# An encoder trunk on one core: bias reads moved in a queue, factors in two parts, wider products in two places

## The chip, the core and the metric

The kernel runs on one core of a Trainium2 chip. The core's engines work side by side, each through its own queue of instructions in a fixed order: TensorE (PE, products; its weight loads are listed as PEld), VectorE (DVE), ScalarE (ACT), GpSimd (POOL) and SyncE (SP), which issues nearly all transfers. Engines wait for each other by semaphores. Products write to eight banks of 128×512 fp32; everything else works in an on-chip memory of 128 partitions. The metric is the device time of one execution in microseconds, the median over runs.

## The reference

512 tokens of 1024 channels pass through two layers, each a mixer and an MLP, each with a norm ahead and a residual behind it, all in fp32, and then a last RMSNorm.

```python
for i in range(DEPTH):                      # two layers
    h = h + mixer_i(rms_norm(h, g_mix[i]))
    h = h + (relu(rms_norm(h, g_mlp[i]) @ w_in[i]) ** 2) @ w_out[i]     # 1024 -> 4096 -> 1024
out = rms_norm(h, norm_final_g)
```

Mixer 0 is attention in dilated windows: 16 heads of 64 channels in three groups (6 heads with dilation 1, 5 with 4, 5 with 16), with a bias by relative position. Each head's output is multiplied, token by token, by a factor that depends on the log-sums of all three groups, and then by w_o. Mixer 1 is differential attention: 8 heads with two softmaxes over all 512 keys, whose difference weights v; then a norm per head and w_o.

## The kernel before

**Products.** Every large product is made of three in a reduced fp32 form: both operands are split into a high and a low part, and `mm3` (L167 to L169) adds hi·hi, hi·lo and lo·hi. The activations lie with channels on the partitions, the 512 tokens along the columns. In `linear_steps` a 128×128 block of weights is held and 512 tokens stream past it. Where the tokens are to end up on the partitions (layer 1's v in `values1`, and `m_end`, the last chunk of the last MLP) it is the other way round: 128 tokens are held and 256 columns of weights stream.

**Weights** come in units of 1 MB, 128 × 8 × 256 or 128 × 4 × 512. `fetch` issues one transfer on SP (L153), casts it in two halves to the high part on ACT (L156, `whi`), and subtracts for the low part on DVE (L157, `wlo`). The raw, high and low tiles have two buffers each; `next_w` hands out one unit and fetches the next. The units' order is one list for the whole program. The first two units come in sixteen small loads (L316, L321), one per 128 channels as x arrives. While these are on their way PE computes idle products of an identity (L130, `WARM` of them).

**Order.** Each engine's order is set when the program is built, by a scheduler that follows the program and its dependences; `tc.high_priority()` moves work ahead and `tc.issue_after(x)` keeps an instruction behind another.

**Layer 0.** The bias lies as one row per head in a table `fd` in DRAM, and `hankel` (L425) reads it with overlapping rows: B0 for the 6 heads of the first group (128×6×256), B1 for the 10 others. `softmax_block` (L475 on DVE adds the bias and finds the minimum, L477 on ACT the exponential) follows the logits. Heads go in pairs, p = 0 to 7; pairs 0 to 2 make logits in split form (L349, L350), pairs 3 to 7 ("class logits", L493) from the 64 rows of one head each, `lo64` and `hi64`, four blocks to a head. `values0` makes v and the weighted sums (L541 to L555, O). The sums of the groups go through DRAM and back (L617, L618, `exS`, `allN`), `head_factors` makes a factor per head and token, one transposition brings them to 64 rows (L624, L626), they are written to DRAM (L627, `fac`) and read back spread over 64 partitions per head (L633, `fB`). L641 multiplies O by them, L649 and L650 split the result (`oh`, `ol`), and w_o follows.

**Layer 1.** `qk1` and `values1` make q, k and v, two heads at a time (j = 0 to 3). `woven` steps through the attention of the heads (`attend1`) and takes 1.5 steps of `fill`, the q, k and v of later heads, per step. An attention block of 128 queries: logits, L816 (DVE) and L819 (ACT) softmax, the difference, transpositions (L835), a copy to `aT` (L837, ACT), and the product with v (L844); there are 8 × 4 blocks. `wo1_first` and `wo1_last` apply w_o (b_w_o) in two parts of heads.

**The last stage.** `m_end` turns h to tokens on partitions (L716), adds the products per 256 columns and 128 tokens (L724), squares and sums (L726), multiplies by the norm's gains (L728; on POOL for the first three quarters, `gB`), and in the last quarter adds the four sums (L731, L732), takes the power −1/2 on POOL (L734), scales (L736 on ACT, L738 on DVE) and writes out (L737, L739).

Of the kernel before, what the change touches and what calls it, by code (L numbers as in the profile page):

```python
# [14 lines left out]
ALU = mybir.AluOpType  # L15
# [13 lines left out]
WARM = 14  # L29
# [53 lines left out]
def tile_encoder(ctx: ExitStack, tc: tile.TileContext, x, rel_bias, gains, norm_final_g,  # L83
# [57 lines left out]
    units, ready = [], []  # L141
# [4 lines left out]
    def fetch():  # L146
# [6 lines left out]
        nc.sync.dma_start(raw, w[r0:r0 + kt * P, c0:c0 + ncol].rearrange("(k p) c -> p k c", p=P))  # L153
        for i in range(2):
            c = slice(i * ncol // 2, (i + 1) * ncol // 2)
            nc.scalar.copy(hi[:, :, c], raw[:, :, c])  # L156
            nc.vector.tensor_sub(lo[:, :, c], raw[:, :, c], f32(hi[:, :, c]))  # L157
# [13 lines left out]
    def linear_steps(ct0, kt, ncol, xs, on_out, bank=None, hooks=(), hold=None):  # L171
# [8 lines left out]
        for c in range(ncol // P):  # L180
            s = slice(c * P, (c + 1) * P)
            ps = (bank or acc_tile)()
            for k in range(kt):
                mm3(ps, hi[:, k, s], lo[:, k, s], xh[k], xl[k], k == 0, k == kt - 1)
                n += 1
                if n in hooks:
                    hooks.pop(n)()
                yield
# [99 lines left out]
    for j in range(4):  # L288
        for part in range(3):
            qkv_unit(b_w_qkv, part, j)  # L290
# [157 lines left out]
    hankel(B0, 0, 6, E_G0 + 64, 256)  # L448
# [150 lines left out]
    hankel(B1[:, 0:5, :], 6, 5, E_G1, P)  # L599
    hankel(B1[:, 5:10, :], 11, 5, E_G2, P)  # L600
# [18 lines left out]
    head_factors(allS, [(sS, 0, 5, 1), (sS, 5, 10, 2)])  # L619
    head_factors(allN, [(sN, 0, 6, 0)])  # L620

    fac = dram.tile([64, P], F32, name="fac")
    T = t_tile()
    nc.tensor.transpose(T[0:64, 0:P], sA.rearrange("p h b -> p (h b)"), ident)  # L624
    fT = l0p.tile([64, P], F32, name="fT", bufs=1)
    nc.scalar.copy(fT, T[0:64, 0:P])  # L626
    nc.sync.dma_start(fac, fT)  # L627
    F = []
    for pp in range(4):
        f = l0p.tile([P, 2, SEQ], F32, tag="ptn", name="fB", bufs=4)  # L630
        for hh, rows in enumerate((lo64, hi64)):
            a = fac[0:1, 0:1]
            nc.sync.dma_start(f[rows], bass.AP(tensor=a.tensor, offset=a.offset + (4 * pp + hh) * SEQ,  # L633
                                               ap=[[0, 64], [2 * SEQ, 2], [1, SEQ]]))
        F += [f[:, 0, :], f[:, 1, :]]
# [3 lines left out]
    oh_, ol_ = [], []  # L639
    for p in range(8):  # L640
# [10 lines left out]
        oh_.append(hi)  # L651
        ol_.append(lo)
# [9 lines left out]
    for c in range(4):  # L662
        run(linear_steps(2 * c, KT, 256, (oh_, ol_), on, bank=wide))
# [4 lines left out]
    def mlp(i, nm, nxt, last=False):  # L668
# [32 lines left out]
        def m_end(c):  # L701
# [6 lines left out]
            for q in range(4):  # L708
                cs = slice(q * 256, (q + 1) * 256)
                hi, lo = next_w()  # L710
                for half in range(2):
                    T = t_tile().rearrange("p (u c) -> p u c", u=2)
                    for u in range(2):
                        for e in range(2):
                            b = 2 * half + u
                            nc.tensor.transpose(T[:, u, e * P:(e + 1) * P], hT[2 * q + e][:, b * P:(b + 1) * P], ident)  # L716
                    nc.scalar.copy(hN[:, 2 * half:2 * half + 2, cs], T)
                for b in range(NB):
# [4 lines left out]
                    h = hN[:, b, cs]  # L723
                    nc.vector.tensor_add(h, h, ps)  # L724
                    sq = mp.tile([P, 256], F32, tag="sqN", name="sqN")
# [271 lines left out]
```

## Time and profile before

| | |
|---|---|
| runs | 1213.69 us median of 3 (1213.35 to 1214.45) |
| profiled execution | 1211.44 us, span 1209.7 us |
| mean granted clock of TensorE | 0.997 |
| busy | PE 1191.5, PEld 1005.9, DVE 629.3, ACT 500.8, POOL 87.4 us |
| transfers | 117.85 MB, 97 GB/s over the span |

A row of a group or of the timeline has the start (or none), the time, the engine, the line, the operation, and its output and inputs by name; in square brackets stands how long the engine had been idle before it and what it waited for. Products overlap, so the start of one to the start of the next tells what one costs, not its own duration. "Granted clock" is the share of full speed that TensorE was given.

### The profile page before, as it was taken

To read this page: it belongs to the slowest core of one execution; us is meant where nothing else is said; L and a number is where in the kernel's file an instruction comes from. 1 tells how busy PE (TensorE), PEld (TensorE's weight loads), DVE (VectorE), ACT (ScalarE), POOL (GpSimd) and SP (SyncE) were. 2 spreads that over 40 slices of the span, in tenths; PEclk is the share of its full clock that TensorE was granted. 3 is DMA by queue.
4 is the path that set the end of the run, shared out by engine and by line. 5 is a ranking of instruction groups with operands and counts; after the bars stand their busy time and mean duration, and the time that the engine had idled before them with its cause. 6 is when DMAs were issued, how large, how long until landed. Compare 5 with 4: busy or idle time off the path is not lost.

```text
span 1209.7 us, 15193 instructions
## 1 busy us (share of the span) xinstructions
PE 1191.5 (99%) x6093; PEld 1005.9 (83%) x6093; DVE 629.3 (52%) x1052; ACT 500.8 (41%) x923; POOL 87.4 (7%) x145
## 2 busy tenths in 40 slices
PE   9999999999999999999999999999999999999997
PEld 7788877888888888888888898987888888888897
DVE  5684465744433434335478668675644344334333
ACT  5462434534412313313367667655444133123133
POOL 0000000300000000001101121213200000000012
PEclk9999999999999999999999999999999999999999
DMA  7632124333233322333432233222323332233311
GB/s 227 118 105 58 57 72 131 105 105 97 79 103 105 105 80 94 105 105 99 121 105 89 86 123 101 72 80 85 96 82 104 105 105 83 91 105 105 100 41 70
DMA packets 108710, 117.85 MB, mean 97 GB/s; under 512 B 4847, under 2 KB 101295, under 8 KB 108591
## 3 DMA queue, kind: packets, MB, share of 16 engines
q1 hardware_dynamic: 108576, 116.61, 30.9%
q8 instruction: 48, 0.79, 0.3%
q0 software_dynamic: 64, 0.27, 0.1%
q14 instruction: 22, 0.18, 0.1%
HBM read 114.60 MB, written 2.27 MB: 97 GB/s over the span
## 4 chain that ended last, share of the span: by engine, by line
PE 94%; DMA 3%; DVE 1%; ACT 1%; issue 0%; SPq 0%; POOL 0%; POOLq 0%; ACTq 0%; DVEq 0%
PE acc L169 15%; PE acc L168 15%; PE acc L167 15%; PE s_ps L168 13%; PE s_ps L167 13%; PE s_ps L169 13%; PE o_ps L844 2%; DMA raw<-in_a_w_qkv_dram 2%; PE s_ps L349 1%; PE s_ps L350 1%; PE t_ps L835 1%; PE s_ps L493 1%; PE o_ps L553 1%; DMA fB<-fac 1%; PE t_ps L515 1%; PE t_ps L130 0%
## 5 line engine op out<-in xcount | busy, mean ns | idle before, releaser
L156 ACT CAST whi<-raw 128x1024 fp32r<-128x1024 f32 x188 | 188.3, 1049 | 391.8 <-PE s_ps L168 201.1
L157 DVE TENSOR_TENSOR wlo<-raw,whi 128x1024 fp32r<-128x1024 f32 x188 | 224.6, 1232 | 28.4 <-ACT whi L156 27.7
L168 PE MATMUL acc<-Al,whi 128*128 128x512 f32 x472 | 185.8, 394 | 0.0
L167 PE MATMUL acc<-Ah,whi 128*128 128x512 f32 x472 | 185.3, 393 | 0.0
L169 PE MATMUL acc<-Ah,wlo 128*128 128x512 f32 x472 | 184.8, 391 | 0.0
L167 PE MATMUL s_ps<-Ah,whi 128*128 128x512 f32 x352 | 137.3, 391 | 0.0
L168 PE MATMUL s_ps<-Al,whi 128*128 128x512 f32 x352 | 137.2, 390 | 0.0
L169 PE MATMUL s_ps<-Ah,wlo 128*128 128x512 f32 x352 | 136.9, 390 | 0.0
L169 PEld LDWEIGHTS acc<-Ah,wlo 128*128 128x128 f32 x472 | 88.7, 188 | 18.1
L167 PEld LDWEIGHTS acc<-Ah,whi 128*128 128x128 f32 x472 | 88.7, 188 | 17.9
L168 PEld LDWEIGHTS acc<-Al,whi 128*128 128x128 f32 x472 | 88.7, 188 | 17.9
L685 ACT ACTIVATE u<-u 128x512 f32<-128x512 f32 x64 | 40.0, 628 | 96.6 <-DVE u L684 95.9
L694 DVE TENSOR_TENSOR h<-h,s_ps 128x512 f32<-128x512 f32 x33 | 22.7, 688 | 108.0 <-PE s_ps L169 108.0
L167 PEld LDWEIGHTS s_ps<-Ah,whi 128*128 128x128 f32 x352 | 66.1, 188 | 14.8 <-ACT nsq L241 0.5
L168 PEld LDWEIGHTS s_ps<-Al,whi 128*128 128x128 f32 x352 | 66.1, 188 | 14.1 <-issue 0.5
L169 PEld LDWEIGHTS s_ps<-Ah,wlo 128*128 128x128 f32 x352 | 66.1, 188 | 13.7
L243 POOL TENSOR_TENSOR nacc<-nacc,nsq 128x512 f32<-128x512 f32 x18 | 27.4, 1524 | 540.1 <-ACT nsq L241 539.6
L684 DVE SCALAR_TENSOR_TENSOR u<-s_ps,rB 128x512 f32<-128x512 f32 x38 | 26.3, 691 | 76.0 <-PE s_ps L169 73.8
L167 PE MATMUL s_ps<-Bh,whi 128*128 128x512 f32 x152 | 59.1, 389 | 0.0
L168 PE MATMUL s_ps<-Bl,whi 128*128 128x512 f32 x152 | 59.1, 389 | 0.0
L169 PE MATMUL s_ps<-Bh,wlo 128*128 128x512 f32 x152 | 59.1, 389 | 0.0
L816 DVE CUSTOM_DVE_ANT_0 p<-s_ps,bias 128x512 f32<-128x512 f32 x64 | 43.3, 688 | 27.9 <-PE s_ps L350 20.8
(238 smaller groups left out, 2240.4 us busy)
## 6 DMA issues: line engine op xcount, KB each, us to landing
raw<-in_mlp_w_in_dram SPq DMA_DIRECT2D x32, 1024.0 KB, 5.3
raw<-in_mlp_w_out_dram SPq DMA_DIRECT2D x32, 1024.0 KB, 5.1
raw<-in_b_w_qkv_dram SPq DMA_DIRECT2D x12, 1024.0 KB, 5.1
raw<-in_a_w_qkv_dram SPq DMA_DIRECT2D x10, 1024.0 KB, 5.2
bias<-fd SPq DMA_DIRECT2D x16, 448.0 KB, 3.6
raw<-in_a_w_o_dram SPq DMA_DIRECT2D x4, 1024.0 KB, 5.2
raw<-in_b_w_o_dram SPq DMA_DIRECT2D x4, 1024.0 KB, 5.1
h<-in_x_dram SPq DMA_DIRECT2D x8, 256.0 KB, 4.5
```

What stands on the lines that cost most here:

```text
L156: nc.scalar.copy(hi[:, :, c], raw[:, :, c])
L157: nc.vector.tensor_sub(lo[:, :, c], raw[:, :, c], f32(hi[:, :, c]))
L167: nc.tensor.matmul(ps, ahi, bhi, start=first, stop=False)
L168: nc.tensor.matmul(ps, ahi, blo, start=False, stop=False)
L169: nc.tensor.matmul(ps, alo, bhi, start=False, stop=last)
L243: eng.tensor_add(self.acc, self.acc, sq)
L349: nc.tensor.matmul(S, q[m][:, qs], k[m][:, ks], start=True, stop=False)
L684: nc.vector.scalar_tensor_tensor(u, ps, 0.0, nm.rB, op0=ALU.max, op1=ALU.mult)
L685: nc.scalar.activation(u, u, AF.Square)
L694: nc.vector.tensor_add(hT[ct], hT[ct], ps)
L816: nc.vector.tensor_tensor_reduce(out=xt, in0=S, in1=bias[h][m][:, b * P:b * P + SEQ], scale=1.0, scalar=3.0e38, op0=ALU.add, op1=ALU.min, ...
L844: marks["PV"] = nc.tensor.matmul(O[:, b, :], aT[:, k, :], v[:, k, es], start=k == 0, stop=k == NB - 1)
```

## The change

Nine edits, none of which changes what is computed:

1. seven idle products instead of fourteen;
2. B0 is read in three transfers of two heads; the third, and both of B1, are tied behind the transfer of the first v weights;
3. in the class logits the two halves are tied to alternate, block by block;
4. the factors are transposed and written in two parts, heads 6 to 15 first; the spreads are sixteen transfers of one head instead of eight of two, and w_o goes through the pairs in the order 3, 4, 5, 0, 1, 2, 6, 7;
5. layer 1's v of j = 0 and 1 is made together by `values01`, with 512 columns and four banks, ahead of the attention; the fill loses v of j = 1, and `woven` takes 1.34 steps of it instead of 1.5;
6. in `m_end` the first 512 columns are made with 512-column products in four banks;
7. there the sum of squares takes its scale in the squaring and loses two small operations to an earlier place, and the last 256 columns take the gains in the scaling;
8. b_w_o's units are cast in four pieces instead of two;
9. the units' list follows: v for j = 0 and 1, and the last chunk's first half, are two units of 128 × 4 × 512 each.

```diff
-WARM = 14
+WARM = 7
...
-    units, ready = [], []
+    units, ready, fetched = [], [], []
...
+        n = 4 if w is b_w_o else 2
...
-        nc.sync.dma_start(raw, w[r0:r0 + kt * P, c0:c0 + ncol].rearrange("(k p) c -> p k c", p=P))
-        for i in range(2):
-            c = slice(i * ncol // 2, (i + 1) * ncol // 2)
+        fetched.append(nc.sync.dma_start(raw, w[r0:r0 + kt * P, c0:c0 + ncol].rearrange("(k p) c -> p k c", p=P)))
+        for i in range(n):
+            c = slice(i * ncol // n, (i + 1) * ncol // n)
...
+                elif i == 0 or c < 3 or q >= 2:
+                    unit(mlp_w_out[i], c * 1024, KT, q * 256, 256)
                 else:
-                    unit(mlp_w_out[i], c * 1024, KT, q * 256, 256)
+                    unit(mlp_w_out[i], c * 1024 + q * 512, 4, 0, 512)
...
+        if j == 0:
+            for half in range(2):
+                unit(b_w_qkv, half * 512, 4, 2 * DM, 512)
...
-    hankel(B0, 0, 6, E_G0 + 64, 256)
+    for h in (0, 2):
+        hankel(B0[:, h:h + 2, :], h, 2, E_G0 + 64, 256)
...
+            last = None
             for b in range(NB):
                 for hh, rows in enumerate((lo64, hi64)):
-                    nc.tensor.matmul(S2[hh][:, b, :], q[rows, b * P:(b + 1) * P], k[rows, (3 - b) * P:(4 - b) * P],
-                                     start=True, stop=True)
+                    with tc.high_priority(), tc.issue_after(last.ins) if last else nullcontext():
+                        last = nc.tensor.matmul(S2[hh][:, b, :], q[rows, b * P:(b + 1) * P],
+                                                k[rows, (3 - b) * P:(4 - b) * P], start=True, stop=True)
...
-    hankel(B1[:, 0:5, :], 6, 5, E_G1, P)
-    hankel(B1[:, 5:10, :], 11, 5, E_G2, P)
+    with tc.issue_after(fetched[-1].ins):
+        hankel(B0[:, 4:6, :], 4, 2, E_G0 + 64, 256)
+        hankel(B1[:, 0:5, :], 6, 5, E_G1, P)
+        hankel(B1[:, 5:10, :], 11, 5, E_G2, P)
...
+    def factors(h0, h1):
+        n = (h1 - h0) * NB
+        with tc.high_priority():
+            T = t_tile()
+            nc.tensor.transpose(T[0:n, 0:P], sA[:, h0:h1, :].rearrange("p h b -> p (h b)"), ident)
+            fT = l0p.tile([40, P], F32, tag="fT", name="fT")
+            nc.scalar.copy(fT[0:n], T[0:n, 0:P])
+        nc.sync.dma_start(fac[h0 * NB:h1 * NB], fT[0:n])
+
+    def spread(*pairs):
+        f = l0p.tile([P, 2, SEQ], F32, tag="ptn", name="fB", bufs=4)
+        for i, p in enumerate(pairs):
+            for hh, rows in enumerate((lo64, hi64)):
+                a = fac[0:1, 0:1]
+                nc.sync.dma_start(f[rows, i, :], bass.AP(tensor=a.tensor, offset=a.offset + (2 * p + hh) * SEQ,
+                                                         ap=[[0, 64], [1, SEQ]]))
+            F[p] = f[:, i, :]
+
     head_factors(allS, [(sS, 0, 5, 1), (sS, 5, 10, 2)])
+    factors(6, 16)
+    spread(3, 4)
     head_factors(allN, [(sN, 0, 6, 0)])
...
+    factors(0, 6)
+    spread(5, 0)
+    spread(1, 2)
+    spread(6, 7)
...
-    for p in range(8):
+    HEADS = (3, 4, 5, 0, 1, 2, 6, 7)
+    for p in HEADS:
...
-        run(linear_steps(2 * c, KT, 256, (oh_, ol_), on, bank=wide))
+        run(linear_steps(2 * c, KT, 256, (oh_, ol_), on, bank=wide, order=HEADS))
...
+            rows_of(0)
+            rows_of(256)
+            banks = [acc_tile(), acc_tile(), s_tile(), s_tile()]
+            for half in range(2):
+                hi, lo = next_w()
+                for b, ps in enumerate(banks):
+                    ts = slice(b * P, (b + 1) * P)
+                    for k in range(4):
+                        d = 4 * half + k
+                        mm3(ps, xh[d][:, ts], xl[d][:, ts], hi[:, k, :], lo[:, k, :], d == 0, d == KT - 1)
+                    if half == 1:
+                        add(b, 0, 512, ps, 0)
...
+                    if q == 2:
+
+                        nc.vector.tensor_scalar(ssq[:, b, 3:4], ssq[:, b, 0:1], ssq[:, b, 1:2], EPS, op0=ALU.add, op1=ALU.add)
+                    else:
                         ms = mp.tile([P, 1], F32, tag="msN", name="msN")
-                        nc.vector.tensor_reduce(ms, ssq[:, b, :], axis=AX.X, op=ALU.add)
-                        nc.vector.tensor_scalar(ms, ms, 1.0 / DM, EPS, op0=ALU.mult, op1=ALU.add)
+                        nc.vector.tensor_add(ms, ssq[:, b, 2:3], ssq[:, b, 3:4])
...
-                        nc.vector.tensor_scalar(ot[:, 512:DM], hN[:, b, 512:DM], r, None, op0=ALU.mult)
+                        nc.vector.scalar_tensor_tensor(ot[:, 768:DM], hN[:, b, 768:DM], r, gB[:, 768:DM],
+                                                       op0=ALU.mult, op1=ALU.mult)
+                        nc.vector.tensor_scalar(ot[:, 512:768], hN[:, b, 512:768], r, None, op0=ALU.mult)
...
+    def values01():
+
+        xh, xl = norm.xs
+        v = [l1p.tile([P, NB, 256], F32, tag="v1", name="v1") for _ in range(2)]
+        banks = [acc_tile(), acc_tile(), s_tile(), s_tile()]
...
-    run(values1(0))
-    fill = chain(*[g for j in range(1, 4) for g in (qk1(j), values1(j))])
-    woven(attend1(fill), fill, 1.5)
+    values01()
+    fill = chain(qk1(1), *[g for j in range(2, 4) for g in (qk1(j), values1(j))])
+    woven(attend1(fill), fill, 1.34)
```

**Where it moves instructions.** On SP at the bias reads, before and after (`fd` is the bias table, `raw` a unit of weights, `raw_676` and `raw_670` the first v's):

```order
L153 DMA raw_396<-in_a_w_qkv_dram 128x8x256
L153 DMA raw_404<-in_a_w_qkv_dram 128x8x256
L382 DMA fd_149<-fsb_155 16x2048
L425 DMA B0_376<-fd_149 128x6x256
L425 DMA B1_506<-fd_149 128x5x128 x2
L153 DMA raw_676<-in_a_w_qkv_dram 128x8x256
L153 DMA raw_746<-in_a_w_qkv_dram 128x8x256
```

```order
L154 DMA raw_390<-in_a_w_qkv_dram 128x8x256
L154 DMA raw_398<-in_a_w_qkv_dram 128x8x256
L391 DMA fd_142<-fsb_148 16x2048
L434 DMA B0_369<-fd_142 128x2x256 x2
L154 DMA raw_670<-in_a_w_qkv_dram 128x8x256
L434 DMA B0_369<-fd_142 128x2x256
L434 DMA B1_500<-fd_142 128x5x128 x2
L154 DMA raw_741<-in_a_w_qkv_dram 128x8x256
```

The first v's weights stand behind 512 KB of bias now and ahead of the rest of it; before, all 1408 KB were ahead.

On PE at the class logits of pair 5, before (the second piece of them; three products of the first half stand 16 rows ahead) and after:

```order
L541 MATMUL t_ps_1214<-ident_84,v0_1212 128x128 x4
L526 MATMUL t_ps_1256<-ident_84,psg_1242 128x128
L493 MATMUL s_ps_1283<-k0_1123,q0_1061 128x128 x2
L526 MATMUL t_ps_1256<-ident_84,psg_1242 128x128
L493 MATMUL s_ps_1283<-k0_1123,q0_1061 128x128
L493 MATMUL s_ps_1282<-k0_1123,q0_1061 128x128
L526 MATMUL t_ps_1256<-ident_84,psg_1242 128x128
L493 MATMUL s_ps_1283<-k0_1123,q0_1061 128x128
L526 MATMUL t_ps_1256<-ident_84,psg_1242 128x128
```

```order
L169 MATMUL acc_1128<-Al7_134,whi_1059 128x512
L505 MATMUL s_ps_1277<-k0_1118,q0_1056 128x128
L505 MATMUL s_ps_1278<-k0_1118,q0_1056 128x128
L505 MATMUL s_ps_1277<-k0_1118,q0_1056 128x128
L505 MATMUL s_ps_1278<-k0_1118,q0_1056 128x128
L505 MATMUL s_ps_1277<-k0_1118,q0_1056 128x128
L505 MATMUL s_ps_1278<-k0_1118,q0_1056 128x128
L505 MATMUL s_ps_1277<-k0_1118,q0_1056 128x128
L505 MATMUL s_ps_1278<-k0_1118,q0_1056 128x128
L170 MATMUL acc_1128<-Ah7_126,wlo_1060 128x512
```

The two outputs, one a half, alternate now in one run of eight; before they stood in groups, with transpositions of the sums (L526) and other products between.

On SP at the factors, before and after (`raw` are w_o's weights):

```order
L617 DMA exS_519<-allS_517 512x1x4
L618 DMA allN_516<-exS_519 128x4x4
L153 DMA raw_1941<-in_a_w_o_dram 128x8x256
L627 DMA fac_1602<-fT_1605 64x128
L633 DMA fB_1608<-fac_1602 64x2x512 x2
L633 DMA fB_1611<-fac_1602 64x2x512 x2
L633 DMA fB_1614<-fac_1602 64x2x512 x2
L633 DMA fB_1617<-fac_1602 64x2x512 x2
L153 DMA raw_2011<-in_a_w_o_dram 128x8x256
```

```order
L631 DMA exS_513<-allS_511 512x1x4
L632 DMA allN_510<-exS_513 128x4x4
L154 DMA raw_1949<-in_a_w_o_dram 128x8x256
L645 DMA fac_1569<-fT_1587 40x128
L645 DMA fac_1569<-fT_1610 24x128
L652 DMA fB_1590<-fac_1569 64x512 x4
L652 DMA fB_1613<-fac_1569 64x512 x4
L652 DMA fB_1618<-fac_1569 64x512 x4
L652 DMA fB_1623<-fac_1569 64x512 x4
L154 DMA raw_2019<-in_a_w_o_dram 128x8x256
```

Both writes of the factors stand ahead of the first spread, which is now the first of four issues of one head each.

More of the change, by code (lines that the diff above doesn't have):

```diff
@@ L715, in m_end, with add @@
                             b = 2 * half + u
[L716 to L717 removed]
+                            nc.tensor.transpose(T[:, u, e * P:(e + 1) * P],
+                                                hT[cols // P + e][:, b * P:(b + 1) * P], ident)
+                    nc.scalar.copy(hN[:, 2 * half:2 * half + 2, cols:cols + 256], T)
+            def add(b, c0, n, ps, part):
+                h = hN[:, b, c0:c0 + n]
+                nc.vector.tensor_add(h, h, ps)
+                sq = mp.tile([P, 512], F32, tag="u", name="sqN")[:, 0:n]
+                nc.scalar.activation(sq, h, AF.Square, scale=1.0 / math.sqrt(DM), accum_out=ssq[:, b, part:part + 1])
+                if part < 2:
+                    nc.gpsimd.tensor_mul(h, h, gB[:, c0:c0 + n])
+            rows_of(0)
[10 more added lines that the diff above has]
+                        add(b, 0, 512, ps, 0)
+            for q in range(2, 4):
+                rows_of(q * 256)
+                hi, lo = next_w()
                 for b in range(NB):
```

58 lines of the change are left out of this document (26 added, 32 removed).

## The prediction

> **What bounds the kernel now.** I read the shares of busy time first, then the chain that ended last, then TensorE's waits.
>
> ```profile
> PE 1191.5 (99%) x6093; PEld 1005.9 (83%) x6093; DVE 629.3 (52%) x1052; ACT 500.8 (41%) x923; POOL 87.4 (7%) x145
> ...
> PE 94%; DMA 3%; DVE 1%; ACT 1%; issue 0%; SPq 0%; POOL 0%; POOLq 0%; ACTq 0%; DVEq 0%
> ```
>
> TensorE (PE) is busy 99% of the span and holds 94% of the chain. Time can go in three ways only: fewer or denser products, fewer waits of PE, and what lies before its first and behind its last product. The waits, in us, times, longest:
>
> ```profile
> PE s_ps L349 <- DVE mnN L475: 3.6, 1, 3.6
> PE t_ps L130 <- POOL ident masks.py:199: 2.5, 1, 2.5
> PE o_ps L844 <- ACT aT L837: 2.1, 2, 1.4
> PE s_ps L167 <- ACT oh L649: 1.6, 1, 1.6
> ```
>
> Four places: the first softmax (3.6), the start (2.5), the end of layer 1's attention (2.1), the step from layer 0's attention into w_o (1.6 for one cast of it). I go through the nine edits by what they do to these and to PE's own products. The sum is made against the profiled execution, 1211.44 us; the median of the runs is 1213.69, 2.25 above it, and I add the 2.25 at the end.
>
> **1. Bias reads behind the fourth weights.** SyncE's queue, its landings, and what ACT and DVE then do:
>
> ```profile
> 30.45 3.07 SPq L425 DMA_DIRECT2D B<-fd  x3
> 35.76 25.21 SPq L153 DMA_DIRECT2D raw<-in_a_w_qkv_dram  x3
> ```
> ```profile
> B<-fd SPq DMA_DIRECT2D x1, 768.0 KB, 11.4
> B<-fd SPq DMA_DIRECT2D x2, 320.0 KB, 19.0
> ```
> ```profile
> 57.13 1.99 ACT L156 CAST whi<-raw 128x1024 fp32r<-128x1024 f32 x2 [10.20 <-DMA raw<-in_a_w_qkv_dram]
> ```
> ```profile
> 58.21 2.36 DVE L157 TENSOR_TENSOR wlo<-raw,whi 128x1024 fp32r<-128x1024 f32 x2 [6.89 <-ACT whi L156]
> 60.49 0.35 DVE L475 CUSTOM_DVE_ANT_0 xt<-s_ps,B 128x192 f32<-128x192 f32 x1
> ```
>
> All 1408 KB of bias rows are issued from 30.45, the weights behind them at 35.76, and ACT gets the weights only at 57.13. DVE has the subtraction ahead of the softmax (L475) in its order, so the softmax starts at 60.49 and PE stands 3.6 us. After the change 512 KB of bias (two of the three B0 reads) stand ahead of that unit. By 768 KB in 11.4 us they take 7.6, so they land near 38.5 and the 1 MB of weights some 3 to 5 us later, by about 43. Cast and subtraction end some 15 us earlier, well before 60.49 − 3.6 = 56.9, near which PE begins to wait. The 3.6 goes; with the hops beside it I take 3.75. The rest of the bias (256 + 640 KB) follows the weights and lands near 55 by the 19.0 row; its first reader is the pairs from 84 us on, so 25 us cover it. The next unit of weights stands behind these reads, lands near 60, and is needed at about 70 (an estimate: the unit before it feeds 48 products of 0.227, part 4, from about 58 on).
>
> Behind the stall lies a second loss. The window from its end, columns span, then busy of PE, its loads, DVE, ACT, POOL, then granted clock, DMA share, GB/s:
>
> ```profile
> 61.34:64.75 3.41, 3.41 (x16) 3.35 (x17) 3.30 (x12) 2.40 (x10) 0.00 (x0) 0.50 0.89 290
> ```
> ```profile
> 64.03 0.41 PE L349 MATMUL s_ps<-sp,sp 128*128 128x256 f32 x1
> 64.25 0.41 PE L350 MATMUL s_ps<-sp,sp 128*128 128x256 f32 x1
> ...
> 64.95 0.28 PE L350 MATMUL s_ps<-sp,sp 128*128 128x256 f32 x1
> 65.07 0.28 PE L349 MATMUL s_ps<-sp,sp 128*128 128x256 f32 x1
> ```
>
> The clock granted was 0.50 for 3.41 us, and equal products started 0.22 us apart in it and 0.12 behind it. Work that took 3.41 us takes 3.41 × 0.12/0.21 = 1.95 at full clock: 1.45 go with the stall, **5.2 in all**. Bounds: 5.4, and 0 if the weights still come late. If only the clock's loss is absent in other executions, 3.75.
>
> **2. Class logits in turn.** All L493 products, in eleven windows (the columns are PE and its loads, clock, DMA):
>
> ```profile
> 84.60:85.70 1.10, 1.09 (x8) 0.96 (x8) 1.00 0.82 174
> ...
> 156.50:157.70 1.20, 1.12 (x16) 0.97 (x16) 1.00 0.00 0
> ...
> sum 10.00, PE 9.50 PEld 7.71; mean PE 0.86 PEld 0.70
> ```
>
> Eight products of one half (64 rows) alone take 1.09; sixteen with the halves in turn take 1.12, since the two halves run side by side. Five pairs are 80 products: 9.50 us now, 5 × 1.12 = 5.6 if every pair alternates, plus 0.3 for one stray that the order leaves apart in one pair. Of the 3.6 that is left I take off 0.2 for modelled ends that overlap the next product. PE has no idle time there to hide in, so **3.4** (bounds 2.8 and 3.8).
>
> **3. Factors in two parts.** The road from the factors to w_o:
>
> ```profile
> 179.92 0.51 SPq L627 DMA_DIRECT2D fac<-fT  x1
> 184.57 5.57 SPq L633 DMA_DIRECT2D fB<-fac  x8
> ```
> ```profile
> fB<-fac SPq DMA_DIRECT2D x8, 256.0 KB, 5.5
> ...
> fac<-fT SPq DMA_DIRECT2D x1, 32.0 KB, 4.6
> ```
> ```profile
> 189.64 1.29 DVE L641 TENSOR_TENSOR fB<-o,fB 128x512 f32<-128x512 f32 x2 [6.12 <-DMA fB<-fac]
> ```
>
> ```profile
> 180.00:204.00 24.00, 21.25 (x129) 16.06 (x129) 14.87 (x18) 10.55 (x15) 0.00 (x0) 1.00 0.62 165
> ```
>
> The write takes 4.6, the spread 5.5, and DVE waits for it until 189.64. In the window (columns as above) PE is idle for 24.00 − 21.25 = 2.75. In the new order both writes stand ahead of the first spread on SyncE, and the first part's transposition is only four products (0.9 us) ahead of the second's, so the first spread starts perhaps 1 us earlier. The spreads are 128 KB instead of 256 KB and the first pair's lands sooner: another 0.6. Against it sixteen issues stand where eight stood; only the first four matter to the first product, and w_o's order starts with those pairs. **1.6**; bounds 0 (the write's own 4.6 is what lasts) and 2.75 (all of the idle time).
>
> **4. 512 columns instead of 256**, in layer 1's v and in the last stage. In each, 192 products become 96. From the chain of waits, two blocks of transpositions with 96 products of 256 columns between them, and from the timeline twenty starts of 512:
>
> ```profile
> 1152.89 0.87 PE t_ps L716 x8
> ...
> 1165.28 0.87 PE t_ps L716 x8
> ```
> ```profile
> 1099.68 0.39 PE L167 MATMUL s_ps<-Ah,whi 128*128 128x512 f32 x1
> ...
> 1103.99 0.39 PE L168 MATMUL acc<-Al,whi 128*128 128x512 f32 x1
> ```
>
> (1165.28 − 1152.89 − 0.87)/96 = 0.120 each; (1103.99 − 1099.68)/19 = 0.227 each. Two of the one cost 13 ns more than one of the other: 96 × 13 ns = 1.25 a place, **2.5** for both. Bounds 0.5 and 2.6.
>
> The Trainium skill (TensorE: Matmul & The Clock Gate, the section "Wait — 56ns, not 53.3ns?") has a fixed 2.5 ns per product at full clock, which would make it 0.25 a place and 0.5 in all; the rows here show more than five times that, and the rows decide.
>
> Moving 96 products (21.8 us as one block) of v ahead of attention takes 11.5 us of filling work out of it. Stage 640 to 700:
>
> ```profile
> 640.00:700.00 60.00, 60.00 (x368) 53.35 (x367) 46.22 (x96) 40.72 (x91) 11.93 (x27) 1.00 0.34 110
> ```
>
> PE is busy all of the time, DVE 77%, ACT 68%. Taking 11.5 from a stage of some 160 us leaves PE 93% of its work, still above DVE: costed at 0, the cover being the 16 points between 93 and 77; the last rival has the price if it is gone.
>
> **5. The last norm.** Behind the last product (DVE, DVE, POOL):
>
> ```profile
> 1203.51 0.43 DVE L728 TENSOR_TENSOR hN<-hN,gB 128x256 f32<-128x256 f32 x1 [0.63 <-ACT sqN L726]
> 1203.85 0.15 DVE L731 TENSOR_REDUCE msN<-ssq 128x1 f32<-128x4 f32 x1
> ...
> 1204.33 0.54 POOL L734 TENSOR_TENSOR rN<-msN,mhalf 128x1 f32<-128x1 f32 x1 [2.34 <-DVE msN L732]
> ```
>
> From the multiply at 1203.51 to POOL's power at 1204.33 are 0.82; one addition of 0.15 with a hop of the same length is left: 0.5 less. DVE then has two operations where it had one, beside ACT's 512 columns, which end last anyway. **0.5**, bounds 0 and 0.8.
>
> **6. Seven idle products instead of fourteen.**
>
> ```profile
> 2.48 5.40 PE L130 MATMUL t_ps<-ident 128*128 128x128 f32 x28 [2.48 <-POOL ident masks.py:199]
> 7.64 0.48 PE L167 MATMUL s_ps<-Ah,whi 128*128 128x512 f32 x1
> ```
> ```profile
> 6.73 0.71 ACT L321 CAST whi<-raw 128x256 fp32r<-128x256 f32 x2 [1.56 <-DMA raw<-in_a_w_qkv_dram]
> ```
>
> ```profile
> 0.00:6.73 6.73, 4.25 (x20) 4.25 (x21) 1.08 (x5) 2.73 (x5) 1.47 (x7) 1.00 0.67 181
> ```
>
> Idle passes hold PE until 7.64, though the first weights' first cast ends about 7.1. Fourteen passes less and PE begins near 7.2: **0.45** gained, if the clock is full then as it is now. If not (the first rival), 1.0 is lost.
>
> **7. Finer wo casts.**
>
> ```profile
> 815.92 2.00 ACT L156 CAST whi<-raw 128x1024 fp32r<-128x1024 f32 x2 [0.91 <-PE acc L168]
> ```
>
> Two casts, 2.00 together, stand ahead of aT's copy (L837), for which PE waits. In the new order all four smaller ones stand in the same row ahead of it, so the split lets nothing through; with half of 1.0 and an estimated 0.1 of fixed cost each, they take 2.4. I take **+0.3**; bounds −2.1 (the wait goes) and +0.8.
>
> **Sum.** −5.2 − 3.4 − 1.6 − 2.5 − 0.5 − 0.45 + 0.3 = −13.35: a profiled time of 1198.1, and a median of 1213.69 − 13.35 = **1200.3**.
>
> **The rivals.**
> *The clock opens a window later at the start* (0.18). In the trace the first 20 idle passes take 4.25/20 = 0.213 each, the other 8 some 0.91/8 = 0.114 (7.64 − 6.73 = 0.91): the clock opened at 6.73, though the column shows 1.00 before it too. 6.73, 61.34 and 64.75 lie on one grid of 3.41 us, whatever the kernel does: (61.34 − 6.73)/3.41 = 16.0. Before the change the window from 3.31 on is full. After it PE stands from about 2.48 + 14 × 0.213 = 5.5 to 7.2, so the window that ends at 6.73 is 63% full; against the rival, the window of the grid that ends at 191.0 holds PE's wait of 1.6 into w_o, so about 53% of it is full, and the clock of 180 to 204 is 1.00. If it opens at 10.14 instead, 2.9 us run at half rate: 1.45 lost, less the 0.45 = +1.0, so 1201.7. The Trainium skill (same page, "Part 1: The HAM clock gate") has the array at half rate until one free-running busy window of 3413 ns has passed, which an idle stretch of 3.0 us need not fill; that speaks for this rival, and its window is the trace's 3.41.
>
> *The factors are no earlier* (0.15): both writes stay ahead of the first spread, and the change does not do what it says there. 1.6 stay: 1201.9.
>
> *The weights stay late* (0.11): transfers share the sixteen DMA engines, and bias rows issued before still hold them when the weights come, or the tied reads delay the next unit. For it: 19.0 us for the second reads. Against it: only 512 KB are ahead now. The 5.2 stay: 1205.5.
>
> *Attention starves* (0.04), the other side: with its fill thinned, PE waits for each query block as it does where fill has run out, 2.1 us in two blocks by the waits, so 1.04 a block. There are 32 blocks (8 heads, 4 blocks). It decides from (13.35 + 2.4)/1.04 = 15 blocks on, half of them: 1216. The missing 11.5 us thin 32 blocks by 0.36 each, and DVE has 0.23 × 5 = 1.1 us of room in a block, which is against it.
>
> **How the numbers follow.** My forecast of 1200.3 has 0.52; its own bounds, with terms failing apart, give 1196 to 1204. The low end of the range adds to −13.35 the upper bounds of factors and wo casts (1.15 and 2.4 more), 1196.8, and a little for the smaller terms: 1196.0. The high end takes in the weights staying late with a little beside it: 1206.5. What is left out is starving and two rivals at once, below 0.2. A change within 0.2% (2.4 us) is about what a measurement of this kernel cannot tell from none. All cases but starving lie more than 7 us below 1213.69, so faster has 0.95, same 0.02, slower 0.03.
>
> **What would show it.** Right: no wait of PE for L475's minimum and a clock of 1.00 around 60 us; L505 (now the class logits' line) busy about 6 us; 96 + 96 starts 0.227 apart; first fB landing near 188. Wrong: rows of clock 0.50 between 7 and 10 us; a wait of PE for aT in many blocks instead of two; a new wait for B1 near 85 us, or for a raw unit near 70.

## The result, and the profile after

The changed kernel takes 1204.36 us (median of 4 runs, 1202.68 to 1205.12) against 1214.07 us (1213.35 to 1215.71): a ratio of 0.9916, interval 0.9899 to 0.9933, or 9.7 us less where 13.4 were forecast. Its profiled execution took 1205.12 us, 6.3 less than that of before. The forecast for it was 1198.1, so 7.0 us are missing there. TensorE is as full as it was (shares of busy time, and the chain that ended last):

```profile
PE 1186.0 (99%) x5888; PEld 992.1 (82%) x5888; DVE 628.2 (52%) x1056; ACT 501.1 (42%) x924; POOL 82.0 (7%) x141
...
PE 95%; DMA 2%; DVE 1%; issue 1%; SPq 0%; ACT 0%; POOLq 0%; POOL 0%; DVEq 0%; ACTq 0%
```

Where the time went shows best in the starts of the same instructions in the two traces, in us from the span's start:

| | before | after | difference |
|---|---|---|---|
| first logits of layer 0 | 47.3 | 48.6 | +1.3 |
| first class logits | 84.6 | 80.4 | −4.2 |
| last product of layer 0's w_o | 238.8 | 233.5 | −5.2 |
| last product with layer 1's v | 825.9 | 821.4 | −4.5 |
| last product of all | 1202.1 | 1196.5 | −5.6 |
| end of the span | 1209.7 | 1203.1 | −6.5 |

The gain comes between the first logits and the class logits (5.5 us, the bias reads), and at the end (2.1). Between the class logits and the end of w_o, where 5.0 more were forecast, 1.0 came. PE's waits name the places (us, times, longest):

```profile
PE t_ps L130 <- POOL ident masks.py:199: 2.5, 1, 2.5
PE t_ps L553 <- DVE v L550: 2.2, 1, 2.2
PE o_ps L915 <- ACT aT L908: 1.6, 1, 1.6
PE t_ps L642 <- DVE sA L602: 0.9, 1, 0.9
PE o_ps L565 <- ACT vn L555: 0.7, 1, 0.7
PE s_ps L358 <- DVE st L887: 0.7, 1, 0.7
PE s_ps L168 <- ACT oh L678: 0.7, 1, 0.7
```

The wait for the first minimum (3.6) is gone. New are one of 2.2 for a v (L553 transposes it) in the factors' stage, one of 0.9 for the second part of the factors, and one of 0.7 in layer 1's attention; three more of 0.4 to 0.6 are left out here.

**The start.** The timeline of PE:

```profile
2.49 3.35 PE L130 MATMUL t_ps<-ident 128*128 128x128 f32 x14 [2.49 <-POOL ident masks.py:199]
6.49 1.22 PE L168 MATMUL s_ps<-Ah,whi 128*128 128x512 f32 x2 [0.65 <-ACT whi L330]
...
8.79 0.63 PE L169 MATMUL s_ps<-Al,whi 128*128 128x512 f32 x1
9.21 0.63 PE L168 MATMUL acc<-Ah,whi 128*128 128x512 f32 x1
```

PE waits 0.65 us for its first weights and then starts products of 512 columns 0.42 us apart until about 11.3, where before they were 0.23 apart from the beginning (the trace's record of the clock begins at 11.9 us here, at 6.7 before). That is the first rival.

**The factors.** SP's queue, then DVE, then PE, then two windows of 3.4 us (columns as in the prediction):

```profile
176.27 10.33 SPq L652 DMA_DIRECT2D fB<-fac  x16
```
```profile
184.02 1.29 DVE L670 TENSOR_TENSOR fB<-o,fB 128x512 f32<-128x512 f32 x2 [2.07 <-DMA fB<-fac]
185.23 1.05 DVE L550 TENSOR_TENSOR v<-acc,rB 128x512 f32<-128x512 f32 x1
```
```profile
186.33 1.12 PE L553 MATMUL t_ps<-ident,v 128*128 128x128 f32 x4 [2.20 <-DVE v L550]
187.38 1.98 PE L565 MATMUL o_ps<-pt,vn 128*64 128x128 f32 x16
```
```profile
182.60:186.00 3.40, 0.88 (x3) 0.30 (x2) 1.98 (x3) 2.00 (x4) 0.00 (x0) 1.00 0.61 210
186.00:189.40 3.40, 3.07 (x21) 2.41 (x21) 3.40 (x6) 2.76 (x5) 0.00 (x0) 0.50 0.42 131
```

The sixteen spreads hold SP for 10.33 us, 0.65 each. DVE stands at the multiplications by the second call of `spread` (L670, 2.07 us of waiting) with the last v (L550) behind them in its order, and PE needs that v after two products of w_o. Where the loss lies can be read from two starts: the first product of w_o comes 7.6 us earlier than before (183.4 against 191.0), the last only 5.2. The stretch with PE 26% busy is followed by one at clock 0.50: the sixteen small products of L565, 1.09 elsewhere, take 1.98.

**Class logits.** Sixteen products in 1.16 us, both halves in turn, for four of the five pairs:

```profile
150.43 1.16 PE L505 MATMUL s_ps<-k,q 64*128 64x128 f32 x16
```

The fifth is split (2 products in 0.48 us, 14 in 1.16); the sum of all is 0.48 + 5 × 1.16 = 6.3 us. Before, it was 9.8 over the whole trace; the prediction's 9.5 leaves out what sticks out of its windows.

**The last norm.**

```profile
1197.86 0.16 DVE L783 TENSOR_TENSOR msN<-ssq 128x1 f32<-128x1 f32 x1 [0.63 <-ACT sqN L752]
1198.10 0.54 POOL L785 TENSOR_TENSOR rN<-msN,mhalf 128x1 f32<-128x1 f32 x1 [2.33 <-DVE msN L783]
```

From DVE's first operation behind the squares to POOL's power are 0.24 us, where 0.82 were.

### The profile page after: what moved, and what is told of

It is laid out like the page before. It is cut to its first block, busy times and chain, and to the rows that moved or that the text cites. A ratio compares the mean times of both kernels' runs of the same rounds, so it can differ in the third digit from the quotient of the medians.

```text
span 1203.1 us, 14799 instructions
## 1 busy us (share of the span) xinstructions
PE 1186.0 (99%) x5888; PEld 992.1 (82%) x5888; DVE 628.2 (52%) x1056; ACT 501.1 (42%) x924; POOL 82.0 (7%) x141
## 4 chain that ended last, share of the span: by engine, by line
PE 95%; DMA 2%; DVE 1%; issue 1%; SPq 0%; ACT 0%; POOLq 0%; POOL 0%; DVEq 0%; ACTq 0%
PE acc L169 15%; PE acc L168 15%; PE acc L170 15%; PE s_ps L168 14%; PE s_ps L170 14%; PE s_ps L169 14%; PE o_ps L915 2%; PE s_ps L358 1%; PE s_ps L359 1%; PE t_ps L906 1%; PE o_ps L565 1%; PE s_ps L505 0%; PE t_ps L527 0%; DMA fac<-fT 0%; DMA raw<-in_a_w_qkv_dram 0%
## 5 line engine op out<-in xcount | busy, mean ns | idle before, releaser
L157 ACT CAST whi<-raw 128x1024 fp32r<-128x1024 f32 (+1 forms) x196 | 189.1, 1014 | 385.6 <-PE s_ps L169 205.3
L158 DVE TENSOR_TENSOR wlo<-raw,whi 128x1024 fp32r<-128x1024 f32 (+1 forms) x196 | 223.4, 1180 | 38.4 <-ACT whi L157 37.9
```

## The experiments

Each gives the median of its runs and that of the kernel before on the same chip. Single runs of one kernel lie up to 7 us apart where the waits depend on when transfers land, so the profiles and the medians are read together.

### The factors

**e1: factors, spreads and the order of pairs as before, the rest as changed.**

```diff
-    factors(6, 16)
-    spread(3, 4)
...
+    T = t_tile()
+    nc.tensor.transpose(T[0:64, 0:P], sA.rearrange("p h b -> p (h b)"), ident)
...
-    HEADS = (3, 4, 5, 0, 1, 2, 6, 7)
```

> The changed kernel with the factors, spreads and w_o's order of pairs as they were before. Theory (the edit turned a gain of 1.6 into a loss: sixteen issues of 0.65 us on SP, and DVE's multiplications that wait for them stand ahead of the last v, for which PE waits 2.2 us, after which the clock drops to 0.50): PE's stall before the first w_o product comes back at about 1.7 us, the wait for v is gone, the clock stays at 1.00, and the time falls by 2 to 4 us against the changed kernel, to 1200.5 to 1202.5. Rival (the stage is bound by the round trip of the factors through DRAM, and lost more only because the earlier edits brought PE there 9 us sooner): PE waits for the spread by 4 us or more, and the time stays at 1204.4 or rises to 1206.

Measured: 1202.81 us (1199.95 to 1206.51) against 1213.92, so 1.5 below the changed kernel, within the spread of both and less than the 2 to 4 expected. From the first logits to the end of w_o the profile is 1.3 us shorter. SP's queue, PE's wait, and DVE at the start of the last factors:

```profile
177.35 5.95 SPq L648 DMA_DIRECT2D fB<-fac  x8
```
```profile
PE t_ps L639 <- DVE sA L602: 1.7, 1, 1.7
```
```profile
170.79 0.17 DVE L590 TENSOR_REDUCE fM<-allN 128x4 f32<-128x12 f32 x1 [1.88 <-DMA allN<-exS]
```

The wait for v and the drop of the clock are gone, but the 1.7 us stand at another place than expected: ahead of the transposition of the factors. There PE now arrives before the factors do, and DVE, which makes them, waits 1.88 us for the groups' sums to come back from DRAM. So in this profile both had a part: the edit cost time, and the sums' round trip through DRAM takes some of what the earlier edits gained.

**e2: only the order on DVE.** The sixteen spreads stay. `vmark[7]` is the multiplication that makes the last v, `ols` are the subtractions for the low parts.

```diff
-    for p in HEADS:
-        nc.vector.tensor_mul(F[p], O[p], F[p])
+    ols = []
+    for i, p in enumerate(HEADS):
+        behind = None if i < 2 else vmark[7] if i < 3 else ols[i - 3]
+        with tc.issue_after(behind.ins) if behind else nullcontext():
+            nc.vector.tensor_mul(F[p], O[p], F[p])
```

> The changed kernel, but the third multiplication by the factors is tied behind the last v on DVE, and each later one behind the low part of the pair three places earlier. Theory (the order on DVE is the cause, not the transfers): the wait of PE for v (2.2 us) is gone, the clock stays at 1.00 in the stage, PE is idle at most 1.5 us between 180 and 195, and the time falls by 2.5 to 4 us to 1200.5 to 1202. Rival (the spreads come too late whatever the order): PE waits for oh or ol of the second and third pair instead, and the time stays within 1 us of 1204.4.

Measured: 1201.86 us (1199.42 to 1203.14), 2.5 below the changed kernel; first logits to end of w_o 3.5 us shorter in the profile. DVE and PE:

```profile
182.46 1.07 DVE L552 TENSOR_TENSOR v<-acc,rB 128x512 f32<-128x512 f32 x1 [1.05 <-PE acc L170]
```
```profile
183.74 1.09 PE L567 MATMUL o_ps<-pt,vn 128*64 128x128 f32 x16
184.76 0.66 PE L555 MATMUL t_ps<-ident,v 128*128 128x128 f32 x4
```

The v now waits for PE's own product and no spread, and PE for no v. With the same transfers the loss is gone, so it was the order on DVE, not the transfers. Outside this stretch the two profiles have the same lengths: 31.8 us from the first logits to the class logits in both, 587.9 and 588.0 from w_o to the last product with v.

**e11: the second part of the factors later.** It stands on e10 (below), which has e2's order; `tmark[4]` is the transposition of pair 4's v.

```diff
-    factors(0, 6)
+    values0(2)
+    factors(0, 6, tmark[4].ins)
     spread(5, 0)
     spread(1, 2)
     spread(6, 7)
-    values0(2)
```

> e10 with the second part of the factors transposed behind the first v of the last four pairs. Theory (PE waits 1.1 to 1.8 us for the second part's factors although it has other work): that wait is gone, the first spread stands ahead of the second write, and the time falls by 0.8 to 1.5 us against e10. Rival (the second write is now behind the wait of the first spread on SP, so the second spread comes some 4 us later): PE waits for oh or ol of the third pair by 1 us or more, and the time is that of e10 or above.

Measured: 1198.29 us (1197.64 to 1199.10) against e10's 1199.27 (1198.87 to 1199.57). SP:

```profile
176.03 2.41 SPq L654 DMA_DIRECT2D fB<-fac  x4
178.49 0.55 SPq L647 DMA_DIRECT2D fac<-fT  x1
179.15 8.30 SPq L654 DMA_DIRECT2D fB<-fac  x12
```

The first spread stands ahead of the second write, and PE's wait for the second part is gone, as expected; 0.4 us of waiting for `ol` came back, which the rival had put at 1 or more. This is the order that "in two parts" promised and the change did not have.

### The bias reads

**e5: the kernel before with this edit alone.**

```diff
-    hankel(B0, 0, 6, E_G0 + 64, 256)
+    for h in (0, 2):
+        hankel(B0[:, h:h + 2, :], h, 2, E_G0 + 64, 256)
...
+    with tc.issue_after(fetched[-1].ins):
+        hankel(B0[:, 4:6, :], 4, 2, E_G0 + 64, 256)
...
```

> The kernel before, with the order of the bias reads of the change and nothing else. Theory: PE's wait of 3.6 us for the first minimum is gone and no window of clock 0.50 lies behind it, so the time falls by 5.2 us or more, to 1208 or 1207 (more, since most runs of the kernel before have a mean clock of 0.994 to 0.995 where the profiled one had 0.997); a smaller wait of 0 to 1.3 us near 65 us can come in its place, for the exponentials behind the cast of the sixth weights. Rival (the weights stay late behind the bias rows): a wait of 3 us or more for the same minimum stays, and the time is within 1 us of 1213.9.

Measured: 1207.98 us (12 runs, 1206.04 to 1212.69) against 1213.36: ratio 0.9957 (0.9945 to 0.9968), 5.4 us. The profiled execution was the slowest of the twelve, and shows what takes the wait's place. ACT, PE, and PE's window behind it:

```profile
63.56 2.00 ACT L156 CAST whi<-raw 128x1024 fp32r<-128x1024 f32 x2 [4.42 <-DMA raw<-in_a_w_qkv_dram]
```
```profile
68.16 0.88 PE L516 MATMUL t_ps<-ident,PN 128*128 128x128 f32 x4 [2.17 <-ACT PN L478]
```
```profile
68.70:72.10 3.40, 3.40 (x12) 2.77 (x13) 3.37 (x14) 2.88 (x13) 0.00 (x0) 0.66 0.83 287
```

The next unit of weights, now behind 896 KB of bias rows, lands at 63.5. ACT waits for it with the exponentials behind the cast, PE waits 2.17 us for the exponentials, and the clock drops again. In the changed kernel's profile the same cast starts at 60.52, in e2's at 59.70, and PE does not wait; in e6, e1 and e4 it starts at 62.14, 62.15 and 62.83, and PE waits 0.5, 0.7 and 1.1 us there. The new wait is there in some executions and not in others.

**e7: three mends at once**: e2's order, fourteen idle products, and the rest of the bias reads behind the next unit too.

```diff
+    values0(0)
     with tc.issue_after(fetched[-1].ins):
         hankel(B0[:, 4:6, :], 4, 2, E_G0 + 64, 256)
...
-    values0(0)
```

> The changed kernel with the multiplications ordered as in e2, fourteen idle products, and the rest of the bias reads tied behind the sixth weights instead of the fifth. Theory (late clock 1.3 us, factors 2.5 us, the wait for exponentials 0 to 1.3 us): no wait for exponentials near 65, first logits at 46.8 to 47.1 us, median 1199 to 1200.5. Rival (fourteen idle products cost what they seemed to in e3, or the bias rows come too late for pair 2 at 76 us): 1202 or more.

Measured: 1201.05 us (1199.69 to 1201.69), half a microsecond above the expected stretch, with no wait for exponentials and runs 2.0 us apart where the changed kernel with fourteen idle products (e3) had 6.9. The cast starts at 57.66 here. The order of the reads was right in kind and one unit too early.

### The idle products

**e3: fourteen again, the rest as changed** (`WARM = 14`).

> The changed kernel with fourteen idle products again. Theory (with seven the clock opens one window of 3.41 us later in most executions, since PE stands idle before its first weights): the first products run at full clock from about 7 us on, the first logits come at 47.1 us instead of 48.4, and the median falls by 0.5 to 1.5 us. Rival (the clock opens in time in most executions and the profiled one was unlucky): the median rises by 0.45 us, or stays.

Measured: 1205.37 us (6 runs, 1202.73 to 1209.64); the median is 1.0 above the changed kernel. Three of the six, at 1206.9 and more, have a mean clock of 0.995 or 0.996, the other three, at 1203.8 and less, of 0.997 to 0.999; so what spreads them, and with them the median, looks like stalls with the clock behind them and not the idle products. The profile is as the theory says: the idle passes end where the first product starts, and it runs at full rate.

```profile
7.35 0.50 PE L168 MATMUL s_ps<-Ah,whi 128*128 128x512 f32 x1
7.69 0.39 PE L169 MATMUL s_ps<-Al,whi 128*128 128x512 f32 x1
7.92 0.40 PE L168 MATMUL s_ps<-Ah,whi 128*128 128x512 f32 x1
```

**e8: as e7, with seven.**

> As e7, with seven idle products as in the change. Theory: the clock opens at 10 to 11 us in the profile, first logits at 47.9 to 48.4 us, and the median lies 1.0 to 1.5 us above that of e7, at 1200.3 to 1201.8. Rival (e3's slower median is due to the idle products themselves): the median is below e7's by 0.45 us or more.

Measured: 1201.82 us (1201.00 to 1203.52), 0.8 above e7. The idle products need not be all of it: in its profile, the slowest of the five, PE also waits 1.7 us for the second part of the factors, where it waits 1.0 in e7, and the clock is 0.50 for a window from 174.8 on.

**e12: as e11, with seven.**

> e11 with seven idle products, as in the change. Theory (in six profiles with seven the first logits came at 47.9 to 48.4 us, in seven with fourteen at 46.5 to 47.9, since the clock opens at 10 to 11 us instead of about 7): first logits at 47.9 to 48.5 us, and the median 0.7 to 1.3 us above e11's, at 1199.0 to 1199.6. Rival (the clock is as often in time, and the passes saved are a gain): the median 0.3 us or more below e11's.

Measured: 1197.56 us (1196.71 to 1199.74), 0.7 below e11, with ranges that overlap, on a chip where the kernel before takes 0.2 less; its profiled execution, first logits at 48.6, is the slowest of its four.

In all seven kernels with seven idle products the profile shows products 0.42 us apart at first, the record of the clock begins at 10.4 to 11.9 us, and the first logits come at 48.0 to 48.6; in the seven with fourteen the record begins at 5.4 to 8.3 and the first logits come at 46.6 to 48.0, a mean of 1.0 earlier. The medians do not follow: seven is 0.8 slower once, 1.0 and 0.7 faster twice. So the late clock is shown for the profiled executions. Whether it is late in the others stays open, and the edit's worth is about 1 us at most either way.

### Layer 1's v and the casts

**e4: v in 256 columns as before, the rest as changed.**

```diff
-    values01()
-    fill = chain(qk1(1), *[g for j in range(2, 4) for g in (qk1(j), values1(j))])
-    woven(attend1(fill), fill, 1.34)
+    run(values1(0))
+    fill = chain(*[g for j in range(1, 4) for g in (qk1(j), values1(j))])
+    woven(attend1(fill), fill, 1.5)
```

> The changed kernel with layer 1's v in 256 columns per head pair and the fill at 1.5 as before; the 512 columns in the last stage stay. Theory (512 columns save 1.25 us of products, and the thinner fill and the casts give about 1.4 of it back as waits at the end of attention): waits of PE between 790 and 825 fall from 3.8 to about 2.4 us, products take 1.25 more, the time stays within 0.7 us of 1204.4. Rival (the waits at the end of attention come from the finer casts alone, as forecast): the waits stay at 3.5 or more and the time rises by 1.25 us to 1205.6.

Measured: 1204.06 us (1202.51 to 1206.56): no difference from the changed kernel, as the theory had it. PE's gaps at the end of attention (starts further apart than usual) fall from 3.8 to 3.0 us and not to 2.4; the wait of 0.7 for `st` is gone.

**e6: w_o's weights cast in two pieces, the rest as changed** (`n = 2`).

> The changed kernel with w_o's weights of layer 1 cast in two pieces. Theory (four pieces take 0.3 to 0.6 us longer ahead of the copy that PE waits for): the waits of PE between 795 and 825 fall from 3.0 us (after the one for the minimum) to 2.4, the time by 0.3 to 0.8 us. Rival (the casts do not matter, the waits come from the thinner fill): they stay at 3.0, the time within 0.3 us.

Measured: 1205.13 us (1204.32 to 1207.24), not faster; but between w_o of layer 0 and the last product with v the profile is 1.7 us shorter. The stage of the factors took it back in this execution: PE's wait for v is longer there by 0.3 us, and it waits 0.5 us for exponentials near 66 us.

**e10: e7 with two pieces.**

> e7 with w_o's weights of layer 1 cast in two pieces. Theory (from the profile of e6, where the stretch from w_o of layer 0 to the last product with v is 586.2 us against 587.9 in the changed kernel): that stretch is 586.2, the median 1.2 to 1.7 us below e7's, at 1199.4 to 1199.9. Rival (the order of layer 1 is made anew with each edit, and the 1.7 came by chance): the stretch is 587 or more, the median within 0.7 us of e7's.

Measured: 1199.27 us (1198.87 to 1199.57), 1.8 below e7, their ranges apart (on two chips, on both of which the kernel before takes 1213.36). With the stage of the factors quiet, the gain shows. The length from the last product of w_o to the last product with v, from all profiles:

| | cast in two | cast in four |
|---|---|---|
| v in 256 columns | 587.1 (before, e5, e9) | 587.9 (e4) |
| v in 512 columns | 586.1 (e6, e10, e11, e12) | 587.9 to 588.2 (after, e1, e2, e3, e7, e8) |

The wider products are worth 1.0 us and the finer casts cost 0.8 alone and 1.8 together with them. The casts themselves, in the changed kernel and in e10:

```profile
810.83 2.18 ACT L157 CAST whi<-raw 128x512 fp32r<-128x512 f32 x4 [0.91 <-PE acc L169]
...
813.75 0.58 ACT L908 COPY aT<-t_ps 128x512 f32<-128x512 f32 x1
```
```profile
805.63 1.99 ACT L157 CAST whi<-raw 128x1024 fp32r<-128x1024 f32 x2 [0.91 <-PE acc L169]
...
808.36 0.58 ACT L913 COPY aT<-t_ps 128x512 f32<-128x512 f32 x1
```

Four pieces take 0.19 longer than two, and the copy starts 2.9 and 2.7 us behind the first cast. PE's waits at the end of attention are 3.2 us in the changed kernel (`aT` 1.6, `st` 0.7, and two of 0.5 and 0.4) and 2.1 in e10 (`aT` alone), which is 1.1 of the 1.8. So most of it is not the casts' own time; that it comes from the order of layer 1's instructions, which the scheduler makes anew, is not shown, and which move of it costs what stays open.

### Class logits alone

**e9: the kernel before with the halves tied in turn.**

> The kernel before with only the class logits tied in turn. Theory: the products of this line are busy 5.9 us instead of 9.5 and the time falls by 3.0 to 3.4 us, to about 1210.2. Rival (what PE gains there it waits again at the factors, which hang on the round trip through DRAM and not on PE): the wait ahead of the first product of w_o grows by 1 us or more, and the time falls by less than 2 us.

Measured: 1209.62 us (1208.05 to 1211.52) against 1213.36: ratio 0.9967 (0.9955 to 0.9980), 3.7 us. PE's waits:

```profile
PE s_ps L349 <- DVE mnN L475: 5.2, 1, 5.2
PE t_ps L130 <- POOL ident masks.py:199: 2.5, 1, 2.5
PE o_ps L846 <- ACT aT L839: 2.1, 2, 1.4
PE t_ps L626 <- DVE sA L592: 1.3, 1, 1.3
```

The rival's wait is there at another place, without its price: PE's wait ahead of w_o's first product (1.6) is gone, and 1.3 us ahead of the factors' transposition have come in its stead. The bias reads are those of the kernel before, and here the wait for the first minimum is 5.2 us, not 3.6, with the clock at 0.50 for 6.8 us behind it (60.0 to 66.8).

## Why the prediction was right or wrong, step by step

- **1, the bias reads: right in size.** 5.2 forecast; 5.4 in e5, 5.5 between the two landmarks. Wrong was the sentence that the next unit "is needed at about 70": its products are, but its cast stands on ACT ahead of exponentials that PE wants at 66, so it is needed by about 61.5 (the cast's start less PE's wait, in e1, e4, e5 and e6) and its cast started at 58.6 (e3) to 63.6 (e5). The first v's weights landed at 43.7 in the changed kernel, as forecast (43); their cast starts 9 us earlier than before and not 15, since ACT is at other casts until 48.3, and that is still in time. (The clock's loss was taken with 0.21 us where its rows show 0.22, which makes it 1.55 instead of 1.45.)
- **2, class logits: right.** 3.4 forecast, 3.5 of busy time in the profile (9.8 to 6.3), 3.7 in e9's medians.
- **3, the factors: the step that failed.** "Sixteen issues stand where eight stood; only the first four matter to the first product": true of the first product, for which PE waits 0.7 us instead of 1.6. But the second four matter to the last v, through DVE's order, and PE needs that v two products of w_o later. The order of PE and DVE at that place was not looked at, only SP's. Forecast 1.6 gained; in the profile some 2.5 lost (the stretch gave 1.0, and the class logits in it 3.5), and e2 is 3.5 shorter there. The rival "no earlier" had the place and stopped at zero; a loss was left out of this term's bounds.
- **4, 512 columns: half right.** In the last stage the stretch from the first transposition to the last product is 1.2 us shorter (1.25 forecast). Layer 1's v gave 1.0 of its 1.25 without the finer casts and nothing with them (the table at e10). DVE and ACT covered the thinner fill, as forecast: attention did not starve.
- **5, the last norm: 0.9 from the last product to the end,** 0.5 forecast. From DVE's first operation to POOL's power it is 0.58 (0.82 to 0.24); the other 0.3 lies behind the power, 5.3 us from the end of the span before and 5.0 after, and its cause stays open.
- **6, the idle products: the first rival** came true in the profile, +1.3 us at the first logits (forecast −0.45). PE is idle from about 5.5 to 6.5 us, and the window of 3.4 us that holds this did not open the clock: in the seven profiles PE's busy time is 76 to 82% of it, while windows of 85, 88 and 90%, filled by idle products alone, opened it in e9, e7 and e3. What misled the chance was the window of 53% into w_o: that one kept an open clock, which is not evidence that a window of 63% would open a closed one. The Trainium skill (TensorE: Matmul & The Clock Gate, the section "Part 1: The HAM clock gate") asks for a busy window of about 3.4 us on a grid that runs free of the kernel; the profiles with seven idle products agree, opening at 10.4 to 11.9 us and never at the same point. The medians show no loss.
- **7, the finer casts: sign right, size wrong.** +0.3 forecast (its own terms, 2.4 against 2.00, give 0.4), 0.8 to 1.8 measured; the four casts took 2.18, not 2.4, so the larger part is not the casts' own time. The fixed cost of 0.1 is borne out (0.19 for two casts more); the half of 1.0 beside it already held half of it.

Added up for the profiled execution: the start missed by 1.75 us, the stretch of class logits and factors by 4.0, attention by 1.7; the bias reads were 0.3 better, and so was the end; with 0.2 outside the span that is the 7.0. The median missed by less, 4.1 us. Of the difference, 0.8 is the profiled execution of after, the slowest of its four, and the rest, 2.25, that of before, which was a good one: in most executions of that kernel the mean granted clock is 0.993 to 0.995, in the profiled one 0.997, which fits a larger loss to the stalls of before than its trace shows. e9's profile shows one such loss (5.2 us and 6.8 at half clock); of the other executions only the mean clock is known.

That the measured time lies inside the range, 1196 to 1206.5, is partly luck. It is above the 1204 that the prediction's own bounds allow. In the profiled execution a late clock and a loss at the factors came together, and the prediction had left two rivals at once out of its range; there was room for them only because its upper end was set by a third, the weights staying late, which did not happen.

The version with the mends of e2, e7 and e11 and casts in two pieces (e11, e12) takes 1197.6 to 1198.3 us, a ratio of 0.987 to before (0.9851 to 0.9888 over both intervals), and beats both kernels.

## What to carry to other kernels

A transfer that is split into more issues changes what stands behind each of them: for each consumer that waits, list what is queued behind it on its engine, and who waits for that. Look at the order of the engine that waits, of the engine it waits for, and of the queue; one of the three is not enough. A wait of two microseconds on TensorE cost its own length and then, where it emptied more than half of a window of 3.41 us, that window's successor at half clock; whether it appears can change from one execution to the next, so one profile neither proves such a stage quiet nor sizes it.

## What the runs showed of the hardware

- A window of 3.4 us in which PE was 26% busy (182.6 to 186.0) was followed by one at 0.50. A window about 53% busy was not, in the kernel before. In all fourteen profiles, on the grid that the record of the clock gives, every fall of the clock ahead of the last stage came behind a window in which PE was busy 0 to 48% (nine of them); two of 48 and 49% were not followed by one, nor was any of 50% or more.
- The way back has another bound. At the start, thirteen windows of 52 to 82% did not open the clock, and those of 85 to 100% did. So a window of 52 to 82% kept an open clock and did not open a closed one. PE's ends are modelled, so these shares are good to some per cent.
- The clock column reads 1.00 at the start even where products run at half rate, since the record behind it begins only where the clock opens; there the distance of starts tells.
- SP takes 0.65 us to issue a spread of 64 × 512 and 0.70 to 0.74 for one of twice the bytes (5.57 us for eight before, 5.95 in e1): halving the transfer does not halve the issue.
